# Weight loads of a recurrent trunk's second layer issued by ScalarE instead of SyncE

## Chip, cores and metric

The kernel runs on one core of a Trainium2 chip. The metric is device time in microseconds, the median of three executions. A profile of one further execution shows where the time of that execution went.

## What is computed

A trunk of two layers over 1024 positions of width 1024, batch 1, in float32. Layer 0 has an RG-LRU group and an HGRN2 group side by side and one output projection. Layer 1 is RWKV-7 time mixing; it is the layer that the change touches. Cut to what matters:

```python
r, k_raw, v = x_r @ w_r, x_k @ w_k, x_v @ w_v        # 1024 x 1024 by 1024 x 2048 each
kk = normalised heads of (k_raw * k_k);  k = k_raw * (1 + (a - 1) * k_a)
for t in positions:                                  # 32 heads of 64
    s_kk  = state @ kk_t
    state = state * w_t - outer(s_kk, kk_t * a_t) + outer(v_t, k_t)
    y_t   = state @ r_t
out = ((groupnorm(y) + bonus) * silu(gate)) @ w_o    # 1024 x 2048 by 2048 x 1024
h = h + out;  return rms_norm(h) * final_g
```

## The kernel before

Each float32 product is made of three passes over split operands (high by high, high by low, low by high). Layer 0 and the gates of layer 1 run first. During layer 0 the kernel splits layer 1's weights into high and low parts and stores them in DRAM (`wd` for the three projections, `wod` for the last one).

The recurrence works in 32 units: 4 quarters of 256 positions by 8 groups of 4 heads. Every unit passes through these stages, and the stages of neighbouring units run interleaved by a hand-written list (`program`):

- `stage_g`: the three projections `kr`, `r`, `v`. Each takes four weight tiles of 512 KB (`w_kr`, `w_r`, `w_v`), so 12 loads a unit. `piece` asks for a tile three tiles ahead; five buffers (tag `wt`) turn over.
- `stage_a`: decays and scaled keys; it makes the chunks' matrices `am` and stores parts of them to DRAM (`nd<-am`, L1039, 8 small transfers a unit).
- `stage_i`: reads them back in another layout (`nb<-nd`, L1070, 4), inverts triangular blocks in 31 steps on VectorE (L1080 to L1086), stores the inverse (`xd<-xi`, L1089) and reads it back transposed (`x<-xd`, L1093, 4).
- `stage_v`, `stage_l`: values; the inverse is completed (`x` transposed at L1124, copied at L1129, product `pl`).
- `stage_s`: the state recurrence of the unit's four chunks (`p`, `ph`, `py`; copies `uv`, `t`, `ysb` on ScalarE).
- `stage_n`: group norm and gate (`gt` loaded by ScalarE at L1234), result stored (`y1d<-gt`, L1245).

The last projection is `outs`, once for each half of the positions. Its tiles `w_o` come from `weights1` through the same `load_parts`; each half takes 32 of them. The first half runs under the last units of the recurrence, the second half at the end.

SyncE (SP) only issues transfers. ScalarE (ACT) computes and also issues some: `cum` (L974), `a` (L976), `gt` (L1234), the operands of the last projection (L1260) and the residual (L1293). Both work their list in order: an instruction that waits holds all that stand behind it. The order of each list is set by a planner at build time, which places an instruction when its operands and buffers are free by its own model of time; matmuls alone are pinned to the order in which the program names them (`pin`, L882). Each transfer counts on one of eight semaphores that SP and ACT use in turn, so a transfer also waits until the one eight issues earlier has landed.

Of the kernel before, what the change touches and what calls it, by code (L numbers as in the profile page):

```python
# [9 lines left out]
F32 = mybir.dt.float32  # L10
# [21 lines left out]
def trunk_kernel(ctx: ExitStack, tc: tile.TileContext, I, out, dbg=None):  # L32
    nc = tc.nc
# [884 lines left out]

    def load_parts(src, name):
        t = wp[0].tile([P, 2, 2, TQ], F32R, tag="wt", bufs=5, name=f"w_{name}")  # L920
        nc.sync.dma_start(t.bitcast(F32), src)
        return t

    def piece(i):

        while len(loaded) < min(i + 4, len(order_w)):
            j, p_, q = order_w[len(loaded)]
            loaded.append(load_parts(wd[p_][j][q], ("kr", "r", "v")[j]))
        return loaded[i][:, 0], loaded[i][:, 1]

    def weights1(dq, kp):
        ts = [load_parts(wod[dq][kp * 2 + q], "o") for q in range(2)]
        return [[t[:, w, k] for t in ts for k in range(2)] for w in range(2)]
# [488 lines left out]
```

## Time and profile before

| | |
|---|---|
| median of 3 runs | 2766.95 us (2766.32 to 2776.49) |
| profiled execution, its own time | 2771.17 us |
| its span, first to last instruction | 2769.4 us |
| mean granted TensorE clock | 0.972 |
| TensorE (PE) busy | 2549.4 us, 92% |
| VectorE (DVE) busy | 1728.9 us, 62% |
| ScalarE (ACT) busy | 1226.1 us, 44% |

Busy time counts computation alone: issuing a transfer or waiting for a semaphore is not in it. The recurrence runs from about 1170 us to about 2500 us of the span.

### The profile page before, as it was taken

What the parts mean: (1) busy time and instruction counts of PE and PEld (TensorE: products, weight loads), DVE (VectorE), ACT (ScalarE), POOL (GpSimd) and SP (SyncE); (2) the same over time, 40 slices, a digit from 0 to 9 for tenths busy, and PEclk for the clock granted to TensorE, in tenths of its full rate; (3) what the DMA queues carried; (4) which work ended last, traced back from release to release, by engine and by line L of the source; (5) the groups of instructions that cost most, each with busy time, mean ns of one, the idle gap of its engine ahead of it and who ended that gap; (6) DMA issues with size and microseconds to landing.
All of it is one profiled execution on the core that took longest, in us unless ns stands there. A gap on an engine that the chain in (4) does not pass through costs nothing.

```text
span 2769.4 us, 56914 instructions
## 1 busy us (share of the span) xinstructions
PE 2549.4 (92%) x22203; PEld 2214.3 (80%) x22203; DVE 1728.9 (62%) x4058; ACT 1226.1 (44%) x2439; POOL 654.7 (24%) x648
## 2 busy tenths in 40 slices
PE   7999999999999989997988999889998899998988
PEld 6777878788998766586887888778887788887988
DVE  5466566557657586245787676777767777677221
ACT  5466555555444455433345343453434434443221
POOL 2355444451116450111112011121111211110001
PEclk9999999999999999898999999999999999999999
DMA  6576666674564567685667576666765667666574
GB/s 202 170 254 223 217 212 224 222 255 141 190 192 137 178 198 223 207 293 177 191 210 225 183 221 191 201 203 210 227 198 189 208 204 221 202 211 186 170 266 151
DMA packets 531232, 566.50 MB, mean 205 GB/s; under 512 B 237745, under 2 KB 420242, under 8 KB 530962
## 3 DMA queue, kind: packets, MB, share of 16 engines
q1 hardware_dynamic: 473906, 481.50, 55.4%
q10 hardware_dynamic: 56192, 79.19, 8.7%
q8 instruction: 174, 2.85, 0.4%
q0 software_dynamic: 864, 2.18, 0.2%
q14 instruction: 96, 0.79, 0.1%
HBM read 428.52 MB, written 134.22 MB: 203 GB/s over the span
## 4 chain that ended last, share of the span: by engine, by line
PE 42%; DMA 17%; DVE 15%; issue 8%; ACT 6%; POOL 5%; SPq 4%; ACTq 0%; DVEq 0%; POOLq 0%
PE g L882 12%; PE pa L882 3%; DMA wd<-ht 3%; PE acc L882 3%; PE ph L882 3%; PE p L882 3%; POOL ht L382 2%; SPq L1093 2%; DVE xi L1086 2%; DVE itmp L1084 2%; PE py L882 2%; DMA y1d<-gt 2%; DMA x<-xd 2%; DMA nb<-nd 2%; SPq L1070 2%
## 5 line engine op out<-in xcount | busy, mean ns | idle before, releaser
L882 PE MATMUL g<-x,w_kr 128*128 128x256 f32 x1536 | 243.1, 301 | 8.2 <-DMA w_kr<-wd 8.2
L882 PE MATMUL g<-x,w_r 128*128 128x256 f32 x1536 | 247.1, 298 | 2.3 <-DMA w_r<-wd 2.3
L882 PE MATMUL g<-x,w_v 128*128 128x256 f32 x1536 | 232.7, 301 | 12.4 <-DMA w_v<-wd 12.3
L1086 DVE TENSOR_TENSOR xi<-xi,itmp 128x60 f32<-128x60 f32 (+21 forms) x864 | 222.5, 258 | 24.0
L382 POOL TENSOR_TENSOR ht<-ht 128x512 fp32r<-128x512 f32 x128 | 191.7, 1508 | 183.3 <-ACT ht L381 136.4
L1084 DVE TENSOR_TENSOR itmp<-xi,nb 128x60 f32<-128x60 f32 (+21 forms) x864 | 220.5, 255 | 22.5
L882 PEld LDWEIGHTS g<-x,w_kr 128*128 128x128 f32 x1536 | 206.6, 197 | 27.6 <-issue 19.5
L882 PEld LDWEIGHTS g<-x,w_v 128*128 128x128 f32 x1536 | 198.6, 194 | 32.7 <-DMA w_v<-wd 16.0
L882 PEld LDWEIGHTS g<-x,w_r 128*128 128x128 f32 x1536 | 199.6, 191 | 17.5 <-DMA w_r<-wd 2.5
L249 PE MATMUL acc<-wL_o,y 128*128 128x256 f32 x512 | 144.5, 286 | 7.1 <-DVE wL_o L183 7.1
L247 PE MATMUL acc<-wH_o,y 128*128 128x256 f32 x512 | 139.1, 285 | 4.2 <-ACT wH_o L182 2.0
L250 PE MATMUL acc<-wH_o,y 128*128 128x256 f32 x512 | 142.6, 283 | 0.0
L1074 POOL TENSOR_SCALAR xi<-eye 128x256 f32<-128x256 f32 x32 | 27.5, 861 | 469.0 <-DMA xd<-xi 388.6
L381 ACT CAST ht<-ht 128x512 fp32r<-128x512 f32 x128 | 78.2, 617 | 120.1 <-DMA wd<-ht 55.8
L882 PE MATMUL acc<-w_o,y 128*128 128x256 f32 x960 | 119.8, 288 | 7.3 <-DVE y L1263 4.2
L882 PEld LDWEIGHTS acc<-w_o,y 128*128 128x128 f32 x960 | 118.4, 196 | 8.6 <-DVE y L1263 4.9
L882 PE MATMUL p<-am,t 64*64 64x128 f32 x1024 | 73.6, 285 | 52.1 <-ACT uv L1170 52.1
L997 DVE TENSOR_TENSOR P<-r,lam 128x512 f32<-128x512 f32 x32 | 49.7, 1552 | 113.6 <-ACT r L953 113.6
L1036 DVE TENSOR_TENSOR am<-pa,rwm 128x512 f32<-128x512 f32 x128 | 85.4, 687 | 56.3 <-PE pa L882 56.1
L1217 ACT COPY ysb<-py 128x512 f32<-128x512 f32 x32 | 18.8, 587 | 229.2 <-PE py L882 229.2
L833 POOL TENSOR_TENSOR x<-xm,x 128x512 fp32r<-128x512 f32 x48 | 65.6, 1371 | 210.2 <-ACT x L832 210.2
L199 PE MATMUL gr<-g,wL_g 128*128 128x512 f32 x256 | 105.5, 412 | 9.4 <-DVE wL_g L183 9.3
(391 smaller groups left out, 6614.9 us busy)
## 6 DMA issues: line engine op xcount, KB each, us to landing
w_kr<-wd SPq DMA_DIRECT2D x128, 512.0 KB, 6.7
w_r<-wd SPq DMA_DIRECT2D x128, 512.0 KB, 4.1
w_v<-wd SPq DMA_DIRECT2D x128, 512.0 KB, 3.9
wd<-ht SPq DMA_DIRECT2D x96, 512.0 KB, 3.6
w_o<-wod SPq DMA_DIRECT2D x64, 512.0 KB, 3.4
wod<-ht SPq DMA_DIRECT2D x32, 512.0 KB, 3.6
wst_o<-in_ab_w_out_dram SPq DMA_DIRECT2D x64, 256.0 KB, 3.2
wst_g<-in_c_w_g_dram SPq DMA_DIRECT2D x64, 256.0 KB, 3.0
```

The source lines that it names most:

```text
L199: PE.matmul(ps, l[k], xh[k], start=False, stop=(k == NK - 1))
L247: PE.matmul(o, yH[kt][:, ts_], wh[j], start=(first and tb % 2 == 0), stop=False, skip_group_check=True)
L249: PE.matmul(o, yH[kt][:, ts_], wl[j], start=False, stop=False, skip_group_check=True)
L250: PE.matmul(o, yL[kt][:, ts_], wh[j], start=False, stop=last, skip_group_check=True)
L381: i = S.copy(hl[:, 0].bitcast(F32R), st)
L382: G.tensor_tensor(hl[:, 1].bitcast(F32R), st, hl[:, 0], op=sub)
L833: G.tensor_tensor(xl, x, xh.bitcast(F32), op=sub)
L882: return pin(PE.matmul(*args, **kw))
L1036: V.tensor_tensor(am[q][:, h, :, 0:P], pa.rearrange("p (c t) -> p c t", t=P), rwm.unsqueeze(1).broadcast_to([P, 4, P]), op=mult)
L1070: nc.sync.dma_start(nb[32 * g:32 * g + 32], u["nd"].rearrange("(p x) -> p x", x=2080)[:, 0:2048].rearrange("p (m s) -> p m s", s=64)[:, :, ...
L1084: V.tensor_tensor(t3, xi[:, 0:n, m:m + 1].broadcast_to([P, n, w]), nb[:, m:m + 1, m + 1:32].broadcast_to([P, n, w]), op=mult)
L1086: V.tensor_tensor(xi[:, 0:n, m + 1:32], xi[:, 0:n, m + 1:32], t3, op=add)
```

## The change

All loads through `load_parts` (384 in the recurrence, 64 for the last projection, 512 KB each) are issued by ACT instead of SP. The other transfers stay where they are.

```diff
     def load_parts(src, name):
         t = wp[0].tile([P, 2, 2, TQ], F32R, tag="wt", bufs=5, name=f"w_{name}")
-        nc.sync.dma_start(t.bitcast(F32), src)
+        nc.scalar.dma_start(t.bitcast(F32), src)
         return t
```

## Rows read from the trace of the kernel before

**Rows 1.** The page: span, busy time, share of the span, instructions.
```profile
span 2769.4 us, 56914 instructions
...
PE 2549.4 (92%) x22203; PEld 2214.3 (80%) x22203; DVE 1728.9 (62%) x4058; ACT 1226.1 (44%) x2439; POOL 654.7 (24%) x648
```

**Rows 2.** Two stretches: recurrence, last projection; busy PE, PEld, DVE, ACT, POOL, clock.
```profile
1200.00:2480.00 1280.00, 1161.05 (x13787) 1037.19 (x13786) 921.50 (x2790) 535.79 (x1174) 198.16 (x218) 0.97 0.67 206
2500.00:2760.00 260.00, 243.56 (x2402) 232.21 (x2402) 84.91 (x249) 57.54 (x152) 16.16 (x22) 0.97 0.59 192
```

**Rows 3.** Waits of PE, 1170 to 2480 us: us in total, times, longest.
```profile
PE p L882 <- ACT uv L1170: 61.7, 39, 5.4
PE pl L882 <- DVE x L1124: 35.9, 50, 11.6
PE g L882 <- DMA w_v<-wd: 12.3, 16, 2.0
PE g L882 <- DMA w_kr<-wd: 8.2, 2, 4.9
...
PE g L882 <- DMA w_r<-wd: 2.3, 1, 2.3
```

**Rows 4.** SP in order of time, 1631 to 1647 us (one unit).
```profile
1631.69 2.59 SPq L1039 DMA_DIRECT2D nd<-am  x4
1634.38 0.54 SPq L921 DMA_DIRECT2D w_v<-wd  x1
1635.02 1.69 SPq L1089 DMA_DIRECT2D xd<-xi  x1
1636.81 2.56 SPq L1039 DMA_DIRECT2D nd<-am  x4
1639.46 0.54 SPq L921 DMA_DIRECT2D w_v<-wd  x1
1640.11 2.58 SPq L1093 DMA_DIRECT2D x<-xd  x4
1642.80 2.42 SPq L1070 DMA_DIRECT2D nb<-nd  x4
1645.32 0.81 SPq L921 DMA_DIRECT2D w_v<-wd  x1
```

**Rows 5.** PE in the same unit; in brackets the idle time before and its releaser.
```profile
1644.79 0.24 PE L882 MATMUL pl<-x,am 32*32 32x32 f32 x2 [0.24 <-DVE x L1124]
...
1645.25 0.69 PE L882 MATMUL pl<-x,am 32*32 32x32 f32 x30 [0.22 <-DVE x L1124]
...
1651.26 0.98 PE L882 MATMUL g<-x,w_v 128*128 128x256 f32 x6 [1.45 <-DMA w_v<-wd]
```

**Rows 6.** The transfers that read or write xd, 1200 to 2480 us: duration ns min/median/max.
```profile
L1093 SPq DMA_DIRECT2D x<-xd x116: 583/612/1922, 1253.7 to 2451.7; - x116
L1089 SPq DMA_DIRECT2D xd<-xi x29: 319/367/1690, 1248.1 to 2444.8; - x29
```

**Rows 7.** Waits of DVE, 1170 to 2480 us.
```profile
DVE x L1124 <- DMA x<-xd: 30.3, 15, 6.9
DVE xi L1080 <- DMA nb<-nd: 29.1, 17, 7.5
```

**Rows 8.** DMA issues of the loads: count, KB each, median us to landing.
```profile
w_kr<-wd SPq DMA_DIRECT2D x128, 512.0 KB, 6.7
w_r<-wd SPq DMA_DIRECT2D x128, 512.0 KB, 4.1
w_v<-wd SPq DMA_DIRECT2D x128, 512.0 KB, 3.9
...
w_o<-wod SPq DMA_DIRECT2D x64, 512.0 KB, 3.4
```

**Rows 9.** ACT's own load of a, line L976: its semaphore waits and its issues, ns.
```profile
L976 ACTq EVENT_SEMAPHORE  x32: 17/17/1381, 1143.8 to 2415.1; - x32
L976 ACTq DMA_DIRECT2D a<-ad x32: 326/327/357, 1144.4 to 2415.2; - x32
```

**Rows 10.** Waits of SP, 1170 to 2480 us.
```profile
SPq L921 <- PE g L882: 494.1, 198, 12.4
```

**Rows 11.** Waits of SP, 2480 to 2770 us.
```profile
SPq L921 <- PE acc L882: 82.1, 32, 9.3
```

## The prediction

> **What bounds the kernel now.** I read the page first, for how busy the engines are: PE is busy for 92% of the span, ACT for 44% [rows 1]. A change that only moves issues of transfers cannot shorten PE's work; it can only give back or add idle time of PE. So I then took the two stretches in which the moved loads run. In the recurrence PE is busy 1161.05 of 1280 us, so some 119 us are idle, and ACT is busy 535.79 us; in the last projection PE is busy 243.56 of 260 us [rows 2]. The third view, what PE waited for in the recurrence, says where those 119 us are: 61.7 us for ACT's copy `uv`, 35.9 us for the inverse `x`, and 12.3 + 8.2 + 2.3 = 22.8 us for late weights [rows 3]. These make 120.4 us; the whole game is played over them. The last view is SP in order of time through one unit, with PE beside it [rows 4, 5]. There the reader sees two things. A weight load stands in front of the store `xd<-xi` and a second one in front of its read-back `x<-xd`, the two links on which `pl` on PE depends. And a third `w_v` is issued only behind four `nd`, four `x` and four `nb`, at 1645.32, and PE then stands 1.45 us for it.
>
> **What the change does to each wait.**
>
> *Late weights.* On ACT a load no longer stands behind 2.56 + 2.58 + 2.42 us of small transfers [rows 4]. At best all 22.8 us go [rows 3]; at worst none, where ACT in turn is waiting for PE when the buffer comes free. I take 15 us, two thirds, because ACT has over half of its time idle in this stretch [rows 2] but works in order too.
>
> *The inverse.* Two loads leave the path from `xi` to `x`. By start to start of the neighbours each takes 0.64 us there (1634.38 to 1635.02, 1639.46 to 1640.11 gives 0.65), 1.29 us together [rows 4]. 27 of the 29 units that the stretch shows in full [rows 6] have two such loads, two have one. 29 times 1.29 is 37 us of path. What PE gains is not more than it waits there: 0.24 + 0.22 us in the unit shown [rows 5], 13.3 us over 29 units, and 35.9 us with the few long waits, of which the longest is 11.6 [rows 3]. Ends: nothing (VectorE arrives late at `x` for its own reasons) and 35.9 us. I take 15, near the typical unit.
>
> *The blocks read back for the next inversion.* `nb` stands behind the same loads. DVE waits 29.1 us for it and 30.3 us for `x` [rows 7]; the second is the same delay as PE's wait for `x` and is not counted twice. DVE is busy 921.50 of 1280 us [rows 2], so it is not the bound by itself, and most of its gain is idle time moved elsewhere. Ends 0 and 29.1 us; I take 3. What a small transfer's landing gains when no 512 KB load shares its queue is not shown by any row; it is held inside this upper end.
>
> *The issues on ACT.* 384 + 64 = 448 issues go to ACT [rows 8]. ACT's own issues of such a kind take 0.326 us [rows 9], so 448 times 0.326 = 146 us of ACT's sequencer. The lower end is nothing: ACT's 744 us of idle time in the recurrence [rows 2] covers it. The upper end is all 146 us. They cost where a copy that PE awaits stands behind one: PE waits for `uv` 39 times [rows 3], and one issue in front of each would be 39 times 0.326 = 12.7 us. I take 13, since a unit has 12 loads in some 41 us and the copies come in a dense stretch; without ACT's idle time this would grow toward the upper end.
>
> *Holds on ACT.* A load waits for its buffer (PE done with the tile two before) and for the landing of the transfer eight issues earlier. On SP the first kind lasts 494.1 us in 198 waits in the recurrence, 2.5 us each [rows 10], and 82.1 us in the last projection [rows 11]. On SP this costs little, as only transfers stand behind it. On ACT all its copies and exponentials stand behind it: `uv` and `t` for the state products, `xb` for the inverse, `kr` and `r` for DVE. Lower end: nothing, because PE works in a fixed order and a copy that PE awaits comes later in that order than the tile the load waits for; whoever awaits the copy has then freed the tile already. Upper end: 576 us, the whole of SP's waits made ACT's. The nearest rows are ACT's own loads: of 32 semaphore waits before `a` the median is 17 ns and the worst 1.38 us [rows 9]. I take that worst case once in eight units, 4 times 1.38 = 5.5, rounded to 5 us.
>
> *The last projection.* Loads there are 64, PE waits little [rows 2], and ACT's casts of operands are ahead of need; I put nothing, inside the ends above.
>
> **The sum.** 15 + 15 + 3 gained, 13 + 5 lost: 15 us net. The profiled execution took 2771.17 us (1.8 us around a span of 2769.4 [rows 1]), so it would take 2756. The median of the runs is 4.2 us below it, which gives 2752 us.
>
> The trace shows that an issue by one engine beside one by the other is not slower: ACT's issues stay between 326 and 357 ns over all 32 [rows 9], while SP is issuing for much of the time [rows 4]. The Trainium skill says in "DMA: Bandwidth & Descriptors", section "Issuing engines are not separate DMA queues", that transfers of all issuing engines end up on the same 16 DMA engines and interleave, and that issuing from several saves only the sequencer's time, usually small against the transfer. By that rule the landing times would not improve, and the 3 us for `nb` would be gone: 2755 instead of 2752.
>
> **The rivals.**
>
> *Nothing comes through.* The two loads leave SP, but what ends PE's waits is something else: DVE's 31-step inversion or the chain through `uv`, the largest wait, which the change does not shorten. For it: `uv` alone is 61.7 of the 120 us [rows 3], and time saved before `pl` can be lost again there. Against it: the 1.45 us for `w_v` has nothing else in front of it [rows 5]. It gives 2767 us, within 7 either way. The rule of the Trainium skill cited above ("DMA: Bandwidth & Descriptors") leans to this side.
>
> *All of the waits go.* Late weights, `x` and `nb`: 22.8 + 35.9 + 29.1 = 88 us gained, 18 lost, 70 net: 2697 us. For it: the units are linked, so a transfer that starts earlier lets the next unit's inversion start earlier as well. Against it: DVE and PE both get denser, and PE's list is pinned.
>
> *ACT is held, and it ends slower.* Place: a load on ACT whose buffer or semaphore is late, with `uv` or `xb` behind it. Price: one wait of 2.5 us (494.1 / 198) a unit, half of it reaching PE, 32 times 1.25 = 40 us; with 13 for the issues and 33 gained that is 20 us more, 2787 us. It decides from (33 - 13) / 32 = 0.63 us a unit that reaches PE. For it: the planner places the loads by a model of time that knows nothing of a dense stretch in which SP issues 0.6 us apart and falls behind, and ACT then waits for SP's landings. Against it: the worst wait of ACT's present loads is 1.38 us [rows 9].
>
> **How the numbers follow.** Half a percent, 13.8 us, is about what a measurement of this kernel can tell from no change. The forecast has 0.40; its own range is 2735 to 2764, of which 0.24 lies beyond half a percent faster and 0.16 within. Nothing comes through: 0.18, all within. All waits go: 0.18, faster. ACT held: 0.24, slower. So faster 0.42, within 0.34, slower 0.24. The range reaches into both outer cases: 2705 to 2800 leaves out the far part of either, about 0.18 together; cases of both signs stand in it, so the forecast's own range above says more.
>
> **What would show it.** Right: SP's list from `nd` to `nb` of a unit has no gap for a load and is 1.3 us shorter; PE's waits for weights fall under 10 us and for `x` under 25; PE's waits for `uv` rise by some 10; ACT's busy time stays at 1226 us. Wrong on the issues: waits for `uv` grow by far more than 13 us. Wrong on the holds: semaphore waits of L921 on ACT longer than 1.4 us, with copies behind them, and PE idle for ACT in places where it was not before. The prediction falls if the planner's new order on ACT puts loads in front of the copies that PE awaits in most units, or if the small transfers' landings shorten so much that DVE's waits vanish.

## The result and the profile after

The changed kernel takes 2839.82 us (median of 4 runs, 2831.96 to 2851.14), the kernel before in the same comparison 2771.72 us (4 runs, 2766.32 to 2778.24). The ratio is 1.0232, 95% interval 1.0204 to 1.026: slower by 2.3%, where 2752 us was forecast with a range of 2735 to 2764. The profiled execution took 2841.82 us; its span is 70.7 us longer than that of [rows 1].

The page of the changed kernel first, the lines that answer to [rows 1].

```profile
span 2840.1 us, 56881 instructions
...
PE 2594.1 (91%) x22203; PEld 2263.5 (80%) x22203; DVE 1727.5 (61%) x4058; ACT 1227.1 (43%) x2439; POOL 657.2 (23%) x648
```

The same 22203 instructions of PE are busy 44.7 us longer (2594.1 against 2549.4), and PE's idle time grew by 26.0 us (2840.1 - 2594.1 = 246.0 against 220.0). ACT's and DVE's busy times did not move. The recurrence by windows, as in [rows 2]: busy PE, PEld, DVE, ACT, POOL, granted clock, DMA share, GB/s.

```profile
1200.00:2480.00 1280.00, 1137.32 (x13034) 1022.58 (x13032) 869.63 (x2634) 506.70 (x1109) 192.04 (x206) 0.93 0.66 195
```

In the same 1280 us PE got through 13034 instructions instead of 13787, at a granted clock of 0.93 instead of 0.97. So the loss has two forms, new idle time and slower work. What PE waited for, 1170 to 2560 us (the recurrence ends later now), in place of [rows 3]:

```profile
PE p L882 <- ACT uv L1170: 75.0, 36, 5.3
PE pl L882 <- DVE x L1124: 63.3, 49, 12.1
...
PE g L882 <- DMA w_r<-wd: 2.3, 2, 1.1
```

The waits for `w_v` and `w_kr` are gone from the list, as meant. The waits for the inverse `x` nearly doubled instead of shrinking, and those for `uv` grew. By the program both hang on VectorE's inversion: `x` is its result, and DVE's own `uv` copies share DVE's list with its steps. Its first operation on the blocks read back is L1080; what ended its idle time before it, over the whole run:

```profile
L1080 DVE SCALAR_TENSOR_TENSOR xi<-nb,xi x128: 240/249/1362, 1224.3 to 2618.0; 128x31 f32<-128x31 f32 x32, 128x30 f32<-128x30 f32 x32, 128x29 f32<-128x29 f32 x32, 128x28 f32<-128x28 f32 x32
...
  DMA nb<-nd: 61.2, 19
```

DVE stood 29.1 us for `nb` in the recurrence before [rows 7], 29.8 us over the whole run. The reason is in the transfers. Issues of the changed kernel over the whole run (count, KB each, median us from issue to landing), to set beside [rows 8]:

```profile
w_kr<-wd ACTq DMA_DIRECT2D x128, 512.0 KB, 5.0
w_r<-wd ACTq DMA_DIRECT2D x128, 512.0 KB, 3.5
w_v<-wd ACTq DMA_DIRECT2D x128, 512.0 KB, 3.7
...
nb<-nd SPq DMA_DIRECT2D x128, 128.0 KB, 5.5
...
nd<-am SPq DMA_DIRECT2D x256, 32.0 KB, 3.2
...
xd<-xi SPq DMA_DIRECT2D x32, 128.0 KB, 2.6
x<-xd SPq DMA_DIRECT2D x128, 32.0 KB, 3.6
```

And the small transfers of the kernel before, which stood in no row so far:

```profile
nb<-nd SPq DMA_DIRECT2D x128, 128.0 KB, 3.0
nd<-am SPq DMA_DIRECT2D x256, 32.0 KB, 2.4
...
xd<-xi SPq DMA_DIRECT2D x32, 128.0 KB, 3.7
x<-xd SPq DMA_DIRECT2D x128, 32.0 KB, 3.0
```

The loads land sooner (`w_kr` 5.0 instead of 6.7 us), and so does the store `xd` (2.6 instead of 3.7 us). Of the small transfers shown, the others land later, `nb` most of all: 5.5 instead of 3.0 us. One unit shows how that reaches PE, the one that [rows 4] show before. SP in the changed kernel:

```profile
1647.71 2.58 SPq L1093 DMA_DIRECT2D x<-xd  x4
1650.46 5.48 SPq L1070 DMA_DIRECT2D nb<-nd  x4
```

ACT beside it:

```profile
1650.87 0.33 ACTq L921 DMA_DIRECT2D w_kr<-wd  x1
...
1653.54 0.33 ACTq L921 DMA_DIRECT2D w_kr<-wd  x1
...
1656.55 0.33 ACTq L921 DMA_DIRECT2D w_kr<-wd  x1
...
1658.79 0.33 ACTq L921 DMA_DIRECT2D w_kr<-wd  x1
```

The forecast for SP's list came true: between `x` and `nb` no load stands, and from the unit's first `nd` (at 1640.65 us) to its first `nb` it is 9.81 us instead of 11.11, shorter by the 1.3 us named. But the four `nb`, which took SP 2.42 us to issue before, take 5.48, and while they are in flight ACT issues four loads of `w_kr`. What the DMA engines carried from 1650 to 1662.5 us, by queue (q1 is SP's, q10 ACT's): packets, MB, and the time of the packets as a share of 16 engines. The two shares add up to 103.2%, so packet times overlap.

```profile
q10 hardware_dynamic: 880, 2.96, 65.1%
q1 hardware_dynamic: 5231, 0.87, 38.1%
```

In the kernel before, over 1642 to 1649 us of this unit, everything lay in one queue:

```profile
q1 hardware_dynamic: 5460, 1.40, 92.6%
```

There the loads of `w_kr` were in SP's queue behind `nb`. Now they take most of the engines' time while `nb` is on its way. The end of it is seen at DVE and then PE of the changed kernel (idle time before, and its releaser, in brackets; `issue` means that the profile names none). DVE:

```profile
1662.20 1.10 DVE L1080 SCALAR_TENSOR_TENSOR xi<-nb,xi 128x31 f32<-128x31 f32 x4 [4.34 <-issue]
...
1665.86 0.43 DVE L1169 COPY uv<-p 64x256 f32<-64x256 f32 x1
```

PE:

```profile
1666.74 1.16 PE L882 MATMUL p<-ar,xb 128*128 128x128 f32 x8 [2.48 <-ACT uv L1170]
...
1669.45 1.48 PE L882 MATMUL g<-x,w_kr 128*128 128x256 f32 x6
```

DVE reaches its first L1080 11.74 us after the first `nb` was issued (1662.20 - 1650.46), against 5.13 before (1647.93 in the row below, less 1642.80 [rows 4]). The unit is no exception: over the 32 units this stretch, worked out from the starts in the two traces, has a median of 10.76 us against 5.41. The copy `uv` that DVE owes stands among the inversion's steps on its list, ACT's copy comes after it, and PE stands 2.48 us. Then the second form of the loss shows: six matmuls take 1.48 us. The same six in the kernel before, below DVE's row of that unit:

```profile
1647.93 0.25 DVE L1080 SCALAR_TENSOR_TENSOR xi<-nb,xi 128x31 f32<-128x31 f32 x1 [0.73 <-DMA nb<-nd]
```

```profile
1658.93 0.87 PE L882 MATMUL g<-x,w_kr 128*128 128x256 f32 x6
```

The granted clock in the changed kernel around this gap, in windows (busy PE, granted clock, DMA share, GB/s):

```profile
1656.00:1663.00 7.00, 7.00 (x82) 1.00 1.07 353
1663.00:1667.00 4.00, 1.52 (x14) 1.00 0.19 71
1667.00:1671.00 4.00, 4.00 (x24) 0.66 0.50 173
1671.00:1676.00 5.00, 5.00 (x92) 0.93 0.51 161
```

PE is busy throughout at full clock (2.4 GHz), then for 1.52 of 4 us, and in the 4 us after that, though it is busy in all of them, it gets 0.66: the larger part of that stretch at the lower of its two levels, 1.2 GHz (0.5).

### The profile page after: what moved, and what is told of

Read it like the earlier page. It is cut to its first block, busy times and chain, and to the rows that moved or that the text cites. A ratio compares the mean times of both kernels' runs of the same rounds, so it can differ in the third digit from the quotient of the medians.

```text
span 2840.1 us, 56881 instructions
## 1 busy us (share of the span) xinstructions
PE 2594.1 (91%) x22203; PEld 2263.5 (80%) x22203; DVE 1727.5 (61%) x4058; ACT 1227.1 (43%) x2439; POOL 657.2 (23%) x648
## 3 DMA queue, kind: packets, MB, share of 16 engines
q10 hardware_dynamic: 120704, 314.10, 33.5%
## 4 chain that ended last, share of the span: by engine, by line
PE 50%; DMA 16%; DVE 13%; issue 6%; ACT 6%; POOL 5%; SPq 3%; ACTq 0%; DVEq 0%; POOLq 0%
PE g L882 15%; PE acc L882 4%; DMA wd<-ht 3%; PE pa L882 3%; DMA nb<-nd 3%; PE p L882 3%; DMA x<-xd 3%; PE ph L882 2%; POOL ht L382 2%; PE py L882 2%; SPq L1093 2%; DVE xi L1086 2%; PE gr L199 1%; DVE itmp L1084 1%; SPq L1070 1%
## 5 line engine op out<-in xcount | busy, mean ns | idle before, releaser
L882 PE MATMUL g<-x,w_v 128*128 128x256 f32 x1536 | 257.1, 326 | 0.1
L1086 DVE TENSOR_TENSOR xi<-xi,itmp 128x60 f32<-128x60 f32 (+21 forms) x864 | 230.5, 267 | 22.8
L882 PEld LDWEIGHTS g<-x,w_v 128*128 128x128 f32 x1536 | 225.3, 220 | 17.2 <-issue 14.2
L1084 DVE TENSOR_TENSOR itmp<-xi,nb 128x60 f32<-128x60 f32 (+21 forms) x864 | 197.1, 228 | 22.8
L882 PEld LDWEIGHTS p<-ar,xb 128*128 128x128 f32 x512 | 71.0, 209 | 65.1 <-ACT uv L1170 49.2
L882 PE MATMUL p<-ar,xb 128*128 128x128 f32 x512 | 77.3, 299 | 45.9 <-ACT uv L1170 45.8
L882 PE MATMUL pa<-P,BK 64*128 64x128 f32 x1024 | 111.8, 288 | 5.6 <-DVE BK L1016 3.6
```

What stands on the lines that cost most here:

```text
L882: return pin(PE.matmul(*args, **kw))
L1084: V.tensor_tensor(t3, xi[:, 0:n, m:m + 1].broadcast_to([P, n, w]), nb[:, m:m + 1, m + 1:32].broadcast_to([P, n, w]), op=mult)
L1086: V.tensor_tensor(xi[:, 0:n, m + 1:32], xi[:, 0:n, m + 1:32], t3, op=add)
```

## The experiments

The change does three things at once, so three theories stood against each other. *Side by side*: loads in another queue are served by the DMA engines while `nb` is in flight, `nb` lands late, and DVE and PE follow. *Reordered*: the planner, given another list, put the work of DVE, ACT, POOL and SP in another order, and that order is worse. *Held*: ACT stands at the loads or spends its time on issuing them. To take the second out, most kernels keep the order of the kernel before: each instruction of DVE, ACT, POOL and SP (the moved loads excepted) is chained behind the one that it followed there, without a wait on the chip. PE's order is pinned anyway. With "order kept" this edit is meant:

```diff
     gq.append(outs(1))
     fill(999)
+    for names in orders_of_the_kernel_before:      # DVE, ACT, POOL, SP
+        for a, b in zip(names, names[1:]):
+            tc.add_manual_dep(at[b], a, no_sync, reason="given order")
```

Ratios are against the kernel before on the same chip, whose medians were 2771.76, 2768.75 and 2777.97 us in the three sets of four; each comes with its 95% interval.

### The change in two halves

All loads on ACT, order kept:

> All loads on ACT as in the change, but DVE, ACT, POOL and SP keep the instruction order of the kernel before (the loads fall in between on ACT). Side by side (loads on ACT's queue are served between the small packets of nb, which lands some 4 us later a unit): stays slow, 2815 to 2850, nb from first issue to DVE's first use near 8.8 us as after the change (4.7 before). Reordered (the planner's new order on DVE and ACT costs the time): back to 2755 to 2775. Held (ACT stands at loads): stays slow, with nb near 5 us and PE's waits for uv well over 77 us.

Measured: 2886.30 us, ratio 1.0415 (1.0367 to 1.0462), above both ranges given (2815 to 2850 and 2755 to 2775 us). From the first `nb` issue to DVE's first use it is 9.59 us at the median of the units (5.41 before), near the 8.8 of *side by side*. PE's wait for `uv` is 115.0 us (1170 to 2560 us), which *held* had named too, though with `nb` near 5 us. The other half, loads back on SP, but DVE, ACT, POOL and SP's small transfers in the order that the planner chose for the change:

```diff
-        nc.scalar.dma_start(t.bitcast(F32), src)
+        nc.sync.dma_start(t.bitcast(F32), src)       # and the order of the changed kernel given
```

> The loads back on SP, but DVE, ACT, POOL and SP's small transfers keep the order that the planner chose for the change. Reordered: slow, 2815 to 2850. Side by side: within 20 us of the kernel before, 2755 to 2790, nb near 5 us. Held: near the kernel before too.

Measured: 2804.14 us, ratio 1.0115 (1.0069 to 1.0161), between the ranges of *side by side* and *reordered* and in neither; `nb` lands in 3.1 us. So the loads on ACT are slow without any new order, and slower than with it: the new order, which costs 1.15% with the loads on SP, makes up for some of the loss with the loads on ACT (2839.82 against 2886.30 us, each in its own comparison). *Reordered* is not needed to make the loads on ACT slow, though the new order costs something by itself.

### Which loads

Only one kind on ACT, `name in ("kr",)` or `("r",)` or both `("r", "v")` in this line, first with the planner free:

```diff
-        nc.sync.dma_start(t.bitcast(F32), src)
+        (nc.scalar if name in ("kr",) else nc.sync).dma_start(t.bitcast(F32), src)
```

> Only the w_kr loads (128) on ACT; they are the ones that are issued while nb is under way. Side by side: half or more of the loss, 2800 to 2840, nb at 7 us or more. Held: a third of the recurrence's loads, so a third of the loss, 2785 to 2795, nb near 5 us. Reordered: no forecast, the order is new again.

> Only the w_r loads (128) on ACT; they are issued in the stretch in which SP has no small transfers. Side by side: no loss, 2755 to 2780, nb near 5 us. Held: a third of the loss or more, 2785 to 2800, since ACT's long wait before ar (L1114) stands at a w_r load. Reordered: no forecast.

Measured: `w_kr` alone 2890.07 us, ratio 1.0429 (1.039 to 1.0469), `nb` lands in 4.3 us at the median and is first used 8.59 us after a unit's first `nb` issue (7 us or more had been forecast). `w_r` alone 2824.64 us, ratio 1.019 (1.0149 to 1.023), although `nb` lands in 3.1 us. The first goes the way of *side by side*, but beyond its range of 2800 to 2840 us; the second lies above the ranges of *side by side* and of *held*. Its trace shows at one place what else may cost time. ACT and then PE of the `w_r` kernel:

```profile
1662.51 0.59 ACT L983 ACTIVATE k<-a,kam,prm 128x256 f32<-128x256 f32 x1
1662.66 0.33 ACTq L921 DMA_DIRECT2D w_r<-wd  x1
1663.00 0.59 ACT L983 ACTIVATE k<-a,kam,prm 128x256 f32<-128x256 f32 x1
1663.49 0.36 ACT L1170 COPY uv<-p 64x256 f32<-64x256 f32 x1
```

```profile
1663.90 1.09 PE L882 MATMUL p<-am,t 64*64 64x128 f32 x16 [2.02 <-ACT uv L1170]
```

Both the scaling L983 and an issue stand ahead of the copy that PE awaits. So this run left *reordered* and *held* open for `w_r`, and the single kinds were run again with the order kept:

> Only the loads of w_r are issued by ACT, and the order of DVE, ACT, POOL and SP's small transfers is that of the kernel before. With the planner's own order this took 2825 us with nb landing as before. Reordered: with the old order 2760 to 2780 us. Held: 2810 to 2830 us still. Side by side: no loads of w_r lie beside nb, so 2765 to 2780 us.

> Only the loads of w_v are issued by ACT, order as in the kernel before. The two loads that stood ahead of xd and its read-backs on SP are gone from there. Side by side: the w_v loads lie beside xd and its four read-backs, which are small packets too; x waits grow by 0.5 to 1 us in each unit, while nb stays at 2.4 us: 2775 to 2815 us. Held: 2775 to 2800 us, from the holds of ACT at w_v alone. As I forecast (the loads on SP are what makes x late): x waits fall and the time is 2745 to 2765 us.

> Only the loads of w_kr are issued by ACT; DVE, ACT, POOL and SP's small transfers keep the order of the kernel before. Side by side: these are the loads that lie beside nb, so nb lands in 4 us or more and nearly the whole loss of all loads in the old order is here: 2850 to 2890 us, though w_r (2774 us alone) and w_v (2757 us alone) cost nothing. Held: a third of the issues gives a third of the loss, 2800 to 2815 us.

> The loads of w_r and w_v are issued by ACT, those of w_kr stay on SP, order as in the kernel before. Side by side: none of ACT's loads lies beside nb, nb lands in about 3 us, and the gain of w_v stays: 2745 to 2775 us. Held: twice as many issues as w_v alone, 2770 to 2800 us.

Measured, with `nb`'s landing (min/median/max) and DVE's waits for it at L1080:

| on ACT, order kept | us | ratio (95%) | `nb` landing, us | DVE for `nb`, us |
|---|---|---|---|---|
| none (before) | | 1 | 2.4/3.0/4.9 | 29.8 |
| `w_r` | 2774.29 | 1.0026 (1.0005 to 1.0047) | 2.4/3.0/6.7 | 35.1 |
| `w_v` | 2757.38 | 0.9966 (0.995 to 0.9983) | 2.3/3.2/5.1 | 23.7 |
| `w_r`, `w_v` | 2765.80 | 0.9962 (0.9945 to 0.9979) | 2.2/3.2/4.9 | 28.5 |
| `w_kr` | 2908.24 | 1.0473 (1.0433 to 1.0513) | 2.4/4.8/11.5 | 110.7 |
| all three | 2886.30 | 1.0415 (1.0367 to 1.0462) | 3.1/5.3/11.1 | 112.8 |

`w_r` costs nearly nothing in the old order, so the 1.9% of the free planner was the order (with the issues that it placed), not ACT standing. `w_v` and `w_r` together even gain 0.4%. With these two on ACT, moving `w_kr` as well takes the ratio from 0.9962 to 1.0415: the loss comes with `w_kr`, the loads that lie beside `nb`. One forecast of *side by side* failed: `w_v` lies beside the store `xd` and its read-backs `x`, small transfers too, and was to cost time for it (2775 to 2815 us). It gained, within the 2745 to 2765 us that followed from the prediction; `x` lands in 3.0 us as before and `xd` in 2.4 instead of 3.7. Lying beside a load does not by itself make a small transfer late. An `x` transfer is a quarter of an `nb` (32 against 128 KB); whether that is the reason was not tried.

With `w_kr` alone on ACT the time came out above the range that *side by side* gave (2850 to 2890 us), and PE's waits in the recurrence say why:

```profile
PE g L882 <- DMA w_v<-wd: 106.7, 27, 7.2
PE p L882 <- ACT uv L1170: 48.3, 34, 5.1
```

Here `w_v` is still on SP, behind an `nb` that now takes long, and PE waits 106.7 us for it, while its wait for `uv` is no longer than before. So this kernel loses by another wait than the one with all loads on ACT. My range had left that out.

### Take ACT out of it

The same issues by GpSimd, order kept: ACT has none of them.

```diff
-        nc.scalar.dma_start(t.bitcast(F32), src)
+        nc.gpsimd.dma_start(t.bitcast(F32), src)
```

> The loads are issued by POOL, not by ACT, and the order of DVE, ACT, POOL and SP's small transfers is that of the kernel before. ACT has none of the issues. Side by side: nb lands as late as with ACT's issues, 4 us or more, and the time is 2840 to 2890 us. Held on ACT: nothing holds ACT, 2760 to 2800 us. Reordered: about 2772 us.

Measured: 2905.55 us, ratio 1.0504 (1.0476 to 1.0532), above the range of *side by side*, though ACT issues no load. `nb` lands in 5.8 us and DVE stands 148.7 us for it. *Held* on ACT falls. GpSimd spends some 0.53 us on each issue and now stands at the loads itself, so part of the surplus over 2886 us may be its own; that wasn't separated.

### Take the bytes away

All loads on ACT, order kept, and from the sixth load on each moves an eighth, or half, of its bytes into the same five buffers:

```diff
+        if name == "o" or i < 5:
+            ...                                  # a new tile, which slots keeps
             nc.scalar.dma_start(t.bitcast(F32), src)
+        else:
+            t = slots[i % 5]
+            nc.scalar.dma_start(t.bitcast(F32)[:, 1:2, 1:2, 128:], src[:, 1:2, 1:2, 128:])   # half: [:, 1:2]
```

> The loads of the recurrence are issued by ACT as in the change and DVE, ACT, POOL and SP's small transfers keep the order of the kernel before, but from the sixth load on each moves an eighth of its bytes (a corner of 128 columns; the rest of the tile keeps what an earlier load left, so the weights used are wrong and the result is not the reference's). Issues, semaphores and holds on ACT stay. Side by side (the loads' packets are served between those of nb): nb lands about 2.4 to 3 us after its issue instead of 4.3, and the time falls from 2886 us back to 2760 to 2800 us. Held (ACT stands at the loads): nb's landing does not matter, 2850 to 2890 us. Reordered: the order is the old one, about 2772 us, but then the same kernel with whole loads could not have taken 2886 us.

> All loads of the recurrence from ACT in the old order, but from the sixth on each moves half of its bytes (one of the two halves of the tile; the other keeps what an earlier load left, so wrong weights are used). Side by side: nb's delay goes with the bytes beside it, so its median landing lies between 3.2 us (an eighth) and 5.3 us (all), about 4 us, and the time between 2736 and 2886 us, 2785 to 2835. Held: as with an eighth, 2736 to 2750 us, since only arrival, not issue, would have mattered.

Measured: an eighth 2735.76 us, ratio 0.9884 (0.9866 to 0.9903), below the range of 2760 to 2800 us that *side by side* gave; half 2777.98 us, ratio 1.0002 (0.9989 to 1.0016), below the range of 2785 to 2835 us that *side by side* gave and above the one of *held*. The issues, their number and the order are those of the kernel that took 2886 us. The number of packets in ACT's queue is the same as well (120704); they are shorter, 314.10, 214.74 and 140.23 MB in all for whole, half and an eighth. What moves with them is `nb`. The rows of L1070 in the three kernels (who waited for it, and its landing), the eighth first:

```profile
  DVE xi L1088: 12.4, 11
...
DMA to landing us min/median/max: 2.3/3.2/6.1
```

Half of the bytes:

```profile
  DVE xi L1088: 49.6, 27
...
DMA to landing us min/median/max: 2.3/4.4/7.3
```

All bytes (lines are numbered 8 lower here):

```profile
  DVE xi L1080: 112.8, 29
...
DMA to landing us min/median/max: 3.1/5.3/11.1
```

Landing, DVE's wait and the time grow together with the bytes beside `nb`. The other small transfers follow too (`x` 2.2, 2.6 and 3.4 us, `nd` 2.0, 2.5 and 3.1), so these runs do not single `nb` out, and they do not tell fewer bytes from shorter packets.

### The mirror

All loads on SP as before, order kept, and only the read-backs `nb` go to ACT's queue:

```diff
-            nc.sync.dma_start(nb[32 * g:32 * g + 32], ...)
+            nc.scalar.dma_start(nb[32 * g:32 * g + 32], ...)
```

> The mirror: all loads stay on SP as in the kernel before, and only the four nb read-backs of each unit are issued by ACT, where they wait for nd and hold ACT for up to 3 us. Side by side: what matters is that nb and the loads are in two queues, not which; where a load is in flight nb lands in 4 us or more again. If it were a matter of ACT's queue being served first, nb would land in 2.4 us or less. The time says little, since ACT stands at nb: 2800 to 2900 us.

Measured in two runs: 2840.07 us, ratio 1.0224 (1.0177 to 1.027). Issue and landing of `nb`:

```profile
L1070 ACTq DMA_DIRECT2D nb<-nd x128: 309/644/4318, 1210.2 to 2603.7; - x128
...
DMA to landing us min/median/max: 2.5/5.2/11.3
```

5.2 us again. What makes `nb` land late is not ACT's queue, nor where the loads are, but that `nb` and the loads are in two queues. The time of this kernel is no evidence for the rest of the chain: ACT stands at `nb`, DVE's wait for ACT's copy `r` is 162.3 us (113.6 before), and of DVE's idle time before L1080, 65.6 us in all, the profile puts only 20.1 us down to `nb`.

## Why the prediction was wrong

**The step that failed** is the one for "the blocks read back for the next inversion". I priced `nb` between 0 and a gain of 29.1 us and held that "what a small transfer's landing gains when no 512 KB load shares its queue" lies inside that end. I had bounded the gain and not the loss. One queue had kept the loads of `w_kr` behind `nb`; with two, `nb` shares the engines with them and lands in 5.5 instead of 3.0 us, a loss of 2.5 us at the median of 128 transfers, at the head of a chain through DVE, the inverse and `uv`. In place of a gain of 3 us the whole run has 61.2 us of DVE's waits for `nb` instead of 29.8. That two queues make `nb` late is shown with ACT, with GpSimd and in the mirror. That the time goes with it is shown by the step from 0.9962 to 1.0415 when `w_kr` joins the other loads on ACT, and by the cut bytes. The chain from DVE to PE was followed in one unit.

**The rule that I weighed.** I took from the Trainium skill that transfers of several issuers interleave on the same engines, and read it as saying that landing times would not improve. The same page of the Trainium skill, "DMA: Bandwidth & Descriptors", section "Queues, rings and completion order", states that each DMA engine goes round the queues for which it has work, a packet at a time. The runs agree as far as they go: `nb`'s delay grows with the bytes in the other queue. Read with it, the rule speaks against the change and not for a nought. The packets that the trace counts are unequal: from 1650 to 1662.5 us one of ACT's queue held 3.4 KB (2.96 MB / 880) and took some 148 ns of an engine (65.1% of 16 times 12.5 us, by 880), one of SP's 0.17 KB (0.87 MB / 5231) and 15 ns. If they take turns one by one, a small packet waits ten times its own time, by this estimate. A packet of that page of the Trainium skill is a group of descriptors, typically 9 to 17; whether the trace counts the same packets, and how single turns go, no run here shows.

**Late weights.** The mechanism was right: I gave 15 of 22.8 us, and the list shows 2.3 us for `w_r` in place of 22.8 for all three.

**The inverse.** SP's list got shorter as forecast, but a gain of 15 us is not shown. `w_v` alone on ACT takes the two loads off the path from `xi` to `x` and is 0.34% faster, some 9 us; there PE's wait for `x` is 30.0 instead of 35.9 us (1170 to 2480 us), while its waits for late weights fall from 22.8 to 6.4, so more of the gain seems to lie there. In the whole change PE's wait for `x` went from 35.9 to 63.3 us, as the inversion begins late.

**The issues on ACT.** I priced them at 13 us in front of `uv`. PE's wait for `uv` rose from 61.7 to 75.0 us, by the 13 I had named, but the size says nothing for the step, since DVE's lateness alone lengthens that wait. With an eighth of the bytes all 384 issues of the recurrence stand on ACT and the kernel is 1.2% faster than before, so they cost less than what the loads' leaving SP, together with their smaller size, gives. My reading that an issue by one engine is not slowed by another's rested on ACT's rows alone; SP's own issues of `nb` grew, from 2.5 to 4.6 us for the four of a unit (median over the units, from their durations in the two traces).

**Holds on ACT.** Cheap, as predicted, but not short. The semaphore waits of the loads on ACT, in the changed kernel:

```profile
L921 ACTq EVENT_SEMAPHORE  x348: 17/17/2111, 1168.7 to 2810.6; - x174
```

Half of them last 17 ns; the longest, 2.1 us, passes the 1.4 us that I had set as a sign. These rows, like those of [rows 9] from which I took the price, leave out waits that a load's own instruction carries. ACT in order of time at one such place, and all its waits of this kind:

```profile
1544.17 0.33 ACTq L974 DMA_DIRECT2D cum<-cd  x1
1550.21 0.33 ACTq L921 DMA_DIRECT2D w_r<-wd  x1
1553.23 0.59 ACT L1114 COPY ar<-pr 128x512 f32<-128x512 f32 x1 [9.53 <-PE pr L882]
```

```profile
ACT ar L1114 <- DMA w_r<-wd: 125.4, 16, 11.0
```

For almost 6 us ACT issues and computes nothing; the next load's semaphore wait before 1550.21 lasts 17 ns. But the copy `ar` then starts as soon as PE's `pr` is there (1553.23), and before the change ACT stood 160.8 us for PE at the same copy. That it costs little in all is shown by `w_r` alone in the old order (ratio 1.0026) and by the kernel with `w_r` and `w_v` on ACT (0.9962). The rival "ACT is held" had the sign of the result with the wrong mechanism: with the loads on GpSimd nothing holds ACT and the time is no better.

**What I did not price at all** is PE's clock. I held that a change of issues can only give back or add idle time of PE. PE's busy time grew by 44.7 us for the same instructions, more than its idle time did (26.0 us). Prices in idle time alone left out the larger part. In the unit shown the clock falls to 0.66 after the 2.48 us of idleness; over the recurrence the granted clock stands at 0.93 instead of 0.97. Over the whole span it is 0.948 to 0.952 in all kernels with `w_kr` off SP's queue and whole loads, 0.971 with `w_r` and `w_v` on ACT, and 0.972 before. It is not a matter of `nb` alone: with `w_r` alone on ACT and the planner free it is 0.956, in the mirror 0.965. A smaller slip: I set the 119 us that PE is idle from 1200 us on beside waits counted from 1170 us on; in that window PE is idle for 123.2 us (1310 - 1186.77), which changes nothing.

**What stays open.** The planner's order for the change costs 1.15% with the loads on SP and saves with the loads on ACT; which of its moves does either wasn't traced. Of the 33 us that the kernel with an eighth of the bytes gains, the part of lighter traffic and the part of the loads' leaving SP's list weren't separated. The kernel with half of the bytes has `nb` late (4.4 us) and is as fast as before, so such a gain seems to cover its loss too. No kernel kept `w_kr` on ACT and held only these loads back until `nb` had landed; that would have told `nb` from the other small transfers beside them.

## What to carry to other kernels

Before a bulk transfer is moved to another engine's queue, look at which small transfers it stood behind in the old one: a shared queue is an order, and that order may be what protects a transfer of many small packets on the critical path. Here `w_r` and `w_v` could go (0.4% faster than the kernel before, ratio 0.9962), although `w_v` lies beside small transfers on the path as well, and `w_kr` had to stay in the queue behind `nb`. Which load hurts has to be tried one kind at a time, with the order of all else kept. And price a wait of PE with what its clock loses after it, from rows of the same kernel in which PE had stood idle.

## What was not expected of the hardware

A transfer of 128 KB in small packets lost as much to a neighbour in ACT's queue (5.3 us), in SP's with itself in ACT's (5.2 us) and in GpSimd's (5.8 us), against 3.0 us in one queue with it. The issuing instruction itself grew longer on SP: the four `nb` of the unit shown took 5.48 us instead of 2.42 (4.6 instead of 2.5 at the median of the units). And half of the loads' bytes removed took most of the loss away (1.0002 instead of 1.0415), though `nb`'s landing fell only from 5.3 to 4.4 us: in these kernels the loss goes with how long DVE then stands (49.6 instead of 112.8 us), not in step with the landing.
